# Moving the compressed softmax ahead of the attention loop, and two smaller moves, in a one-core hybrid S5 / sparse-attention layer

## The chip, the cores and the metric

The kernel runs on one core of one Trainium2 chip. The metric is device time in microseconds (us): 828.83 us is the median of three runs before the change (828.5 to 829.4). Matrix products, and the transposes that are done as products, run on TensorE (PE); VectorE is DVE, ScalarE ACT, GpSimd POOL, and SP issues most transfers.

## The reference

One layer on 512 tokens of width 1024, in float32:

```python
n1 = rmsnorm(h, g_mix);  z = n1 @ w_in
y_ssm = s5_mixer(z[:, :512], ...)                      # state space, gelu, glu gate
y_nsa = nsa_mixer(q, kv, gate_logits, ...)             # 8 heads of 64, 2 kv heads
#   o = gates[0]*o_cmp + gates[1]*o_sel + gates[2]*o_win
#   o_cmp: softmax over 31 compressed keys;  o_sel, o_win: causal softmax over 512 keys
merge = sigmoid(z[:, OFF_MERGE:])                      # 2 x 1024 columns
mixed = merge[:, :1024]*(y_ssm @ w_br_ssm) + merge[:, 1024:]*(y_nsa @ w_br_nsa)
h = h + mixed @ w_out
h = h + conv_ffn(rmsnorm(h, g_ffn))                    # 1024 -> 2 x 2816 -> 1024
h = h + sigmoid(rmsnorm(h, g_ple) @ w_ple_gate) * (p @ w_ple_proj)
return rmsnorm(h, g_final)
```

## The kernel before

Every large product is made of three in a reduced format: both operands are split into a high and a low part (`split`: ACT copies the high part, DVE or POOL subtracts it), and `mm3` (lines 83 to 85) issues high x high, high x low and low x high into one PSUM bank. So in the profile each weight tile shows an ACT copy (line 76), a subtraction (line 55) and three products on lines 83, 84, 85. PSUM has eight banks in four rings of two, named `acc`, `s`, `t` and `o`; a tile that is allocated takes the next bank of its ring and waits until that bank's earlier tile has been read. SBUF scratch goes the same way: the tag `mg` of pool `weights` is a ring of two.

The stages stand in program order: norm 1 and the input projections; the S5 quarters; the compressed keys and values (`compress`); the first four merge gates (`gate`, banks `acc`, tiles `pj`); the glu of the S5 output (tiles `glu`, then `sg`, `yg` in ring `mg`, then `y2`); attention; the rest of the merge; `w_out` (tiles `wo`); norm 2 (`norm`, and `to_t`, which transposes the normed rows into banks `nt` and evicts them as `n2h` and `n2l`); the FFN; the gated embedding; the final norm.

Attention is a loop over 16 units (8 heads, 2 branches), each of four steps. `scores` makes products `sps` on line 870, and the softmax runs over DVE, ACT, DVE and POOL (tile `pr`); `transposed` turns it on PE (tile `ptp`, line 885), and ACT and DVE split it into `ph` and `pl`; `values` makes the products on lines 896 to 900 into bank `ops`. The two branches of a head and its compressed part share one bank; at the end `otmp` and `oT` take the head's output out of it. Since these chains are long, a generator `fill` gives PE other work: the remaining 12 merge gates and the 8 products with `w_br_ssm`, 128 pieces (of three products each). `filled(n)` takes `n` pieces, and each step of the loop takes one. What is left is issued after the loop.

The compressed softmax (`compressed`, `compressed_t`) is done once per 128 queries for all heads: 12 products `cs` of 64 columns, eight small DVE and ACT steps on tile `cmps`, two transposes `pct`, and the split into `PTC`, which the first product of each head reads (lines 896, 897). It stands among the scores of the first unit.

The order on each engine is not the order of the text: a scheduler places the instructions by its own model of their times, and within one engine they then run strictly as placed. `tc.issue_after(x)` tells it to place what follows after instruction `x`. After the loop the head outputs `oT` are split into `oS` for the product with `w_br_nsa`; `oT` has one tile for two heads, so three of the four splits are ready before the last two heads are.

Of the kernel before, what the change touches and what calls it, by code (L numbers as in the profile page):

```python
# [9 lines left out]
F32 = mybir.dt.float32  # L10
# [8 lines left out]
P = 128  # L19
T = 512  # L20
# [25 lines left out]
def hybrid_kernel(ctx: ExitStack, tc: tile.TileContext, A, out):  # L46
# [7 lines left out]
    def tt(o, a, b, op, e=V):  # L54
        e.tensor_tensor(o, a, b, op=op)  # L55

    def ts(o, a, s1, s2=None, op0=MUL, op1=None, e=V):
        if op1 is None:
            e.tensor_scalar(o, a, s1, None, op0=op0)
        else:  # L60
            e.tensor_scalar(o, a, s1, s2, op0=op0, op1=op1)  # L61
# [16 lines left out]
    def split(hi, lo, src, e=V):  # L78
        copy(hi, src)
        tt(lo, src, hi, SUB, e)  # L80

    def mm3(ps, lh, ll, rh, rl, start, stop):
        PE.matmul(ps, lh, rh, start=start, stop=False)  # L83
        PE.matmul(ps, lh, rl, start=False, stop=False)  # L84
        PE.matmul(ps, ll, rh, start=False, stop=stop)  # L85
# [15 lines left out]
    def bank(tag, name):  # L101
        return psp.tile([P, 512], F32, tag=tag, name=name, bufs=BANKS[tag])

    def slot(p, tag, shape, dt, name):
        return p.tile(shape, dt, tag=tag, name=name, bufs=1)
# [5 lines left out]
    def small(tag, n=1, bufs=4):  # L111
        return cp.tile([P, n], F32, name=tag, tag=tag, bufs=bufs)
# [73 lines left out]
    def wload(name, ld, row0, c0, kt, c, e=V, keep=None, raw=None):  # L186
        if raw is None:
            raw = wraw(name, ld, row0, c0, kt, c)
        if keep is None:
            hi = pw.tile([P, kt * c], F32R, name="wh", tag="wh").rearrange("p (k c) -> p k c", k=kt)  # L190
            lo = pw.tile([P, kt * c], F32R, name="wl", tag="wl").rearrange("p (k c) -> p k c", k=kt)
        else:
            hi, lo = keep
        split(hi, lo, raw, e)
        return hi, lo
# [619 lines left out]
    def gate_weights(i, e=G):  # L815
        return wload("w_in", INW, 0, OFF_M + i * P, KD, P, e)

    for dt_ in range(4):
        for _ in gate(t1(dt_), gate_weights(dt_, (V, G)[dt_ % 2])):
            pass  # L820

    po = sY.enter_context(pool("att_out", 1, "right"))
    y2 = slot(po, "y16", [P, 2, 4, T], F32R, "y2")
# [4 lines left out]
        split(ys[:, 0, k], ys[:, 1, k], yT[:, k].rearrange("p j c -> p (j c)"))  # L828
    for hc in range(2):
        hi, lo = wload("ssm_w_glu", SSMW, 0, hc * 256, 4, 256, V)  # L830
        for cc in range(2):
            c = 2 * hc + cc
            ps = bank(either(), "glu")
            for k in range(4):
                mm3(ps, hi[:, k, cc * P:(cc + 1) * P], lo[:, k, cc * P:(cc + 1) * P], ys[:, 0, k], ys[:, 1, k],
                    k == 0, k == 3)
            sg, yg = (pw.tile([P, T], F32, name=n, tag="mg") for n in ("sg", "yg"))
            S.activation(sg, ps, AF.Tanh, scale=0.5)
            stt(yg.rearrange("p (c j) -> p j c", j=L), sg.rearrange("p (j c) -> p j c", j=L), 1.0, yT[:, c], ADD, MUL)
            split(y2[:, 0, c], y2[:, 1, c], yg)  # L840


    PTC = slot(pa, "ptc", [P, 2, 2, T], F32R, "PTC")
    oT = slot(py, "y8", [P, 4, T], F32, "oT")
    t1s.append(slot(po, "t16", [P, 4, T], F32, "t1b"))
    sB = ExitStack()
# [56 lines left out]
                copy(tmp, self.ops[64:128])  # L903
                tt(oT[self.r0:self.r0 + 64, self.i], self.ops[0:64], tmp, ADD)

    def compressed(qt):
        qs_ = slice(qt * P, (qt + 1) * P)
        ps = bank("s", "cs")
        for i in range(4):
            mm3(ps[:, 64 * i:64 * i + 64], QT[:, i, 0, qs_], QT[:, i, 1, qs_], KC[:, 0, i // 2], KC[:, 1, i // 2],  # L910
                True, True)
        sc = pt.tile([P, H, NCMP], F32, name="cmps", tag="cmps")
        shc = [P, H, NCMP]
        tt(sc, ps[:, 0:256].rearrange("p (h n) -> p h n", h=H), maskc[:, qt, None, :].to_broadcast(shc), ADD)
        mx, su = small("cmx", H, 2), small("csu", H, 2)
        V.tensor_reduce(mx, sc, AX.X, ALU.max)
        tt(sc, sc, mx[:, :, None].to_broadcast(shc), SUB)
        S.activation(sc, sc, AF.Exp, scale=HD ** -0.5)
        V.tensor_reduce(su, sc, AX.X, ADD)
        V.reciprocal(su, su)  # L920
        tt(su, su, gates[:, qt, 0:8], MUL)
        if qt == 0:
            ts(su, su, rowok)
        tt(sc, sc, su[:, :, None].to_broadcast(shc), MUL)
        return sc

    def compressed_t(qt, sc):
        pc = bank("t", "pct")
        for g in range(2):
            PE.transpose(pc[:, g * P:(g + 1) * P], sc[:, 4 * g:4 * g + 4].rearrange("p h n -> p (h n)"), ident)  # L930
        qs_ = slice(qt * P, (qt + 1) * P)
        split(PTC[:, 0, :, qs_], PTC[:, 1, :, qs_], pc[:, 0:256].rearrange("p (g t) -> p g t", g=2))

    def ssm_branch(dt_, w):
        ps = bank("acc", "br")
        c = (dt_ % 2) * P
# [36 lines left out]
    def filled(n):  # L973

        with tc.issue_after(last_pe()):
            for _ in range(n):
                next(fill, None)

    units = [Unit(h, br) for h in range(H) for br in range(2)]
    units[0].queries(None)  # L980
    scs = {}
    for qt in range(NQ):
        units[0].scores(NQ - 1 - qt)
        scs[qt] = compressed(qt)
        filled(4)
        if qt:
            compressed_t(qt - 1, scs[qt - 1])
    filled(4)
    compressed_t(NQ - 1, scs[NQ - 1])
    pend = None  # L990
    for n, u in enumerate(units):
        nxt = units[n + 1] if n + 1 < len(units) else None
        if nxt:
            nxt.queries(u)
        for i in range(NQ):
            kt = NQ - 1 - i
            u.transposed(kt)
            gate_at = last_pe()
            if pend:
                pend[0].values(pend[1], pend[2])  # L1000
            if nxt:
                nxt.scores(kt)
            pend = (u, kt, units[n - 1] if n else None)
            with tc.issue_after(gate_at):
                next(fill, None)
    pend[0].values(pend[1], pend[2])
    for _ in fill:
        pass

# [4 lines left out]
    w0h = pm_.tile([P, KD, 512], F32R, name="w0h")  # L1014
    hres = slot(cp, "h16", [P, NQ, D], F32, "hres")
    oS = slot(pa, "kv", [P, 2, 4, T], F32R, "oS")
    for i in range(4):
        split(oS[:, 0, i], oS[:, 1, i], oT[:, i])

    mTls = []  # L1020

# [42 lines left out]
    for qp in range(2):  # L1064
        for hf, qt in ((0, 0), (0, 1), (1, 0), (1, 1)) if qp == 0 else ((0, 2), (1, 2), (0, 3), (1, 3)):
            cs = slice(hf * 512, hf * 512 + 512)
            qs_ = slice(qt * P, (qt + 1) * P)
            ps = bank(either(), "wo")
            for k in range(KD):
                mm3(ps, mTh[:, k, qs_], mTl(k)[:, qs_], (w0h, w1h)[hf][:, k],  # L1070
                    w1l[:, k] if hf else w0l[k // 4][:, k % 4], k == 0, k == KD - 1)
            stt(hres[:, qt, cs], ps, 0.5, hres[:, qt, cs], MUL, ADD)
        for j in range(2):
            norm(xg[:, j], hres[:, 2 * qp + j])
        to_t([xg[:, j] for j in range(2)], 2 * qp, 0, lambda x, k, q, w: (n2h, n2l)[x][:, k, q * P:q * P + w])
    sY.close()
    sA.close()

# [451 lines left out]
```

## Time and profile before

| | us |
|---|---|
| three runs, median | 828.83 (828.5 to 829.4) |
| the profiled execution, device time | 829.46 |
| its span on the core | 827.5 |
| PE busy | 807.9 |
| DVE busy | 524.3 |
| ACT busy | 393.5 |
| POOL busy | 255.2 |

Busy time says how long an engine had something in it. On PE the records overlap: a product of 512 columns is shown as 0.39 us, while the next one starts 0.23 us after it. So a wait is read best from the starts of two neighbours, and the idle time that the profile prints in brackets is smaller than the gap between starts. [...]

### The profile page before, as it was taken

Reading aid. Unit: us, or ns where it says so; the run is one execution under the profiler, and the core shown is the slowest. Engines: PE = TensorE matmul, PEld = TensorE weight load, DVE = VectorE, ACT = ScalarE, POOL = GpSimd, SP = SyncE. Lnnn points to the kernel's source line nnn. Section 1 sums busy time; section 2 is a strip of 40 time slices with the busy share of each in tenths; the row PEclk is TensorE's granted clock in tenths of the full one; section 3 lists DMA queues with packets and bytes.
Section 4 is the critical chain, followed back from the end, with each engine's and each line's share of the span. In section 5 each row is a group of like instructions: output and inputs, shape, how many; then the busy total and the mean of one; then the engine's idle time right before and its main releaser. Section 6 shows DMA issues by size and latency. Waiting matters only on the chain. (4 is left out here: it accounts for less than half of the span.)

```text
span 827.5 us, 12241 instructions
## 1 busy us (share of the span) xinstructions
PE 807.9 (98%) x4529; PEld 677.7 (82%) x4529; DVE 524.3 (63%) x1088; ACT 393.5 (48%) x728; POOL 255.2 (31%) x314
## 2 busy tenths in 40 slices
PE   7999999999999999999999999999999999999996
PEld 5877888878888888888898888888888888888885
DVE  6899988377677640685454444444455947898744
ACT  4437553445777753434354444444434433565522
POOL 6595111124555533131032333333333100000411
PEclk9999999999999999999999999999999999999998
DMA  9663322522333423344052333233323342423011
GB/s 244 161 166 103 91 65 65 129 76 77 77 77 83 148 55 96 109 137 118 2 175 80 103 101 100 86 95 103 99 86 95 121 143 93 153 87 117 26 52 51
DMA packets 112001, 83.67 MB, mean 101 GB/s; under 512 B 9665, under 2 KB 97477, under 8 KB 111942
## 3 DMA queue, kind: packets, MB, share of 16 engines
q1 hardware_dynamic: 111262, 81.82, 34.2%
q10 hardware_dynamic: 680, 1.07, 0.3%
q8 instruction: 36, 0.59, 0.3%
q14 instruction: 23, 0.19, 0.1%
HBM read 75.54 MB, written 3.15 MB: 95 GB/s over the span
## 5 line engine op out<-in xcount | busy, mean ns | idle before, releaser
L55 POOL TENSOR_TENSOR wl<-wr,wh 128x1024 fp32r<-128x1024 f32 x39 | 93.6, 2401 | 246.5 <-ACT wh L76 228.5
L76 ACT ACTIVATE wh<-wr 128x1024 fp32r<-128x1024 f32 x90 | 95.2, 1059 | 95.5 <-issue 32.9
L55 DVE TENSOR_TENSOR wl<-wr,wh 128x1024 fp32r<-128x1024 f32 x51 | 66.0, 1294 | 42.7 <-ACT wh L76 42.7
L83 PE MATMUL pj<-n1h,wh 128*128 128x512 f32 x224 | 92.0, 411 | 0.3 <-ACT un L76 0.3
L85 PE MATMUL pj<-n1h,wl 128*128 128x512 f32 x224 | 88.9, 398 | 0.4 <-DVE wl L55 0.4
L84 PE MATMUL pj<-n1l,wh 128*128 128x512 f32 x224 | 88.6, 396 | 0.0
L64 DVE SCALAR_TENSOR_TENSOR cv<-ub,cvp,cv 128x511 f32<-128x511 f32 (+1 forms) x44 | 32.9, 748 | 66.3 <-ACT cv L1193 65.6
L84 PE MATMUL ua<-n2l,wh 128*128 128x512 f32 (+1 forms) x176 | 67.0, 381 | 0.4 <-DVE n2l L64 0.4
L83 PE MATMUL ua<-n2h,wh 128*128 128x512 f32 (+1 forms) x176 | 67.0, 380 | 0.2 <-ACT n2h L166 0.2
L83 PE MATMUL ub<-n2h,wh 128*128 128x512 f32 (+1 forms) x176 | 66.8, 379 | 0.0
L84 PE MATMUL ub<-n2l,wh 128*128 128x512 f32 (+1 forms) x176 | 66.8, 379 | 0.0
L85 PE MATMUL ub<-n2h,wl 128*128 128x512 f32 (+1 forms) x176 | 66.8, 379 | 0.0
L85 PE MATMUL ua<-n2h,wl 128*128 128x512 f32 (+1 forms) x176 | 66.8, 379 | 0.0
L85 PEld LDWEIGHTS pj<-n1h,wl 128*128 128x128 f32 x224 | 42.4, 189 | 10.3 <-DVE wl L55 1.1
L61 POOL TENSOR_SCALAR pr<-pr,su,gates 128x512 f32<-128x512 f32 (+1 forms) x64 | 38.3, 607 | 37.4 <-DVE su L877 36.3
L84 PEld LDWEIGHTS pj<-n1l,wh 128*128 128x128 f32 x224 | 42.7, 190 | 7.9 <-issue 0.6
L83 PEld LDWEIGHTS pj<-n1h,wh 128*128 128x128 f32 x224 | 42.6, 190 | 7.8 <-ACT un L76 0.6
L874 DVE CUSTOM_DVE_ANT_0 pr<-sps,maskb 128x512 f32<-128x512 f32 (+1 forms) x64 | 30.0, 487 | 18.8 <-PE sps L870 9.4
L55 POOL TENSOR_TENSOR wg1l<-wr,wg1h 128x1024 fp32r<-128x1024 f32 x2 | 7.0, 3514 | 111.5 <-ACT wg1h L76 111.5
L55 DVE TENSOR_TENSOR pl<-ptp,ph 128x128 fp32r<-128x128 f32 (+1 forms) x64 | 31.1, 486 | 14.5 <-ACT ph L76 13.8
L76 ACT ACTIVATE ph<-ptp 128x128 fp32r<-128x128 f32 (+1 forms) x64 | 27.6, 433 | 25.7 <-PE ptp L885 25.0
L84 PEld LDWEIGHTS ua<-n2l,wh 128*128 128x128 f32 x176 | 33.1, 188 | 6.8 <-DVE n2l L64 0.6
(495 smaller groups left out, 2078.0 us busy)
## 6 DMA issues: line engine op xcount, KB each, us to landing
wr<-in_w_up_dram SPq DMA_DIRECT2D x44, 512.0 KB, 3.9
wr<-in_w_in_dram SPq DMA_DIRECT2D x28, 512.0 KB, 4.0
b<-in_w_down_dram SPq DMA_DIRECT2D x12, 512.0 KB, 6.2
wr<-in_w_down_dram SPq DMA_DIRECT2D x10, 512.0 KB, 4.5
QQ<-QT SPq DMA_DIRECT2D x16, 256.0 KB, 3.4
wr<-in_w_out_dram SPq DMA_DIRECT2D x8, 512.0 KB, 4.4
wr<-in_w_ple_gate_dram SPq DMA_DIRECT2D x8, 512.0 KB, 5.3
xall<-in_x_dram SPq DMA_DIRECT2D x4, 512.0 KB
```

The lines of the kernel that those rows point to most:

```text
L55: e.tensor_tensor(o, a, b, op=op)
L61: e.tensor_scalar(o, a, s1, s2, op0=op0, op1=op1)
L64: e.scalar_tensor_tensor(o, a, s, b, op0=op0, op1=op1)
L76: S.activation(o, a, AF.Copy)
L83: PE.matmul(ps, lh, rh, start=start, stop=False)
L84: PE.matmul(ps, lh, rl, start=False, stop=False)
L85: PE.matmul(ps, ll, rh, start=False, stop=stop)
L874: V.tensor_tensor_reduce(out=pp, in0=ps[:, :w], in1=maskb[:, T - w:], scale=-(HD ** -0.5), scalar=3e38, op0=ADD, op1=ALU.min, accum_out=nb)
```

## The change

Three parts. `compressed` and `compressed_t` move up, textually unchanged, to the loop over the first four gates: after each gate stand the 12 products and the softmax of one query tile, and the transposes of the tile before; the last transposes come after the first glu weights. The scratch `cmps` changes from a ring of its own in the attention pool to the ring `mg`, and `PTC` is allocated earlier. In attention, the first unit's scores now take three pieces of filling each and no more (12 instead of 20), the last unit takes two pieces a step instead of one, and the splits of `oT` are ordered after the last head's output. In norm 2 the second pair of query tiles is transposed into four different banks (`t`, `t`, `acc`, `o`) instead of the two of ring `t` in turn. Line numbers of the changed program are some 4 to 36 higher: `sps` is on line 906, `pct` on 845, `ptp` on 921, the products of `values` on 932 to 936.

```diff
     for dt_ in range(4):
         for _ in gate(t1(dt_), gate_weights(dt_, (V, G)[dt_ % 2])):
             pass
+        scs[dt_] = compressed(dt_)
+        if dt_:
+            compressed_t(dt_ - 1, scs[dt_ - 1])
...
+    def compressed(qt):
...
+        sc = pw.tile([P, H, NCMP], F32, name="cmps", tag="mg")
...
     for hc in range(2):
         hi, lo = wload("ssm_w_glu", SSMW, 0, hc * 256, 4, 256, V)
+        if hc == 0:
+            compressed_t(NQ - 1, scs[NQ - 1])
...
-        sc = pt.tile([P, H, NCMP], F32, name="cmps", tag="cmps")
...
     for qt in range(NQ):
         units[0].scores(NQ - 1 - qt)
-        scs[qt] = compressed(qt)
-        filled(4)
-        if qt:
-            compressed_t(qt - 1, scs[qt - 1])
-    filled(4)
-    compressed_t(NQ - 1, scs[NQ - 1])
+        filled(3)
...
             with tc.issue_after(gate_at):
-                next(fill, None)
+                for _ in range(1 if nxt else 2):
+                    next(fill, None)
     pend[0].values(pend[1], pend[2])
+    attended = [last(e) for e in (mybir.EngineType.DVE, mybir.EngineType.Activation)]
...
-    for i in range(4):
-        split(oS[:, 0, i], oS[:, 1, i], oT[:, i])
+    with tc.issue_after(attended[0]), tc.issue_after(attended[1]):
+        for i in range(4):
+            split(oS[:, 0, i], oS[:, 1, i], oT[:, i])
...
-        to_t([xg[:, j] for j in range(2)], 2 * qp, 0, lambda x, k, q, w: (n2h, n2l)[x][:, k, q * P:q * P + w])
+        to_t([xg[:, j] for j in range(2)], 2 * qp, 0, lambda x, k, q, w: (n2h, n2l)[x][:, k, q * P:q * P + w],
+             tags=("t", "t", "acc", "o") if qp else "tttt")
```

The program holds the same products and transposes as before. Three places in its order, before and after:

First, PE around the second full group of `cs` in the program before; then the place in the changed one where a group stands between two gates (a line of dots stands for more rows of the same kind).

```order
L85 MATMUL pj<-n1h,wl 128x512
L870 MATMUL sps<-KK,QQ 128x256 x2
L83 MATMUL cs<-KC,QT 128x64
...
L83 MATMUL pj<-n1h,wh 128x512
L930 MATMUL pct<-ident,cmps 128x128 x2
```

```order
L84 MATMUL pj<-n1l,wh 128x512
L845 MATMUL pct<-ident,cmps 128x128 x2
L85 MATMUL pj<-n1h,wl 128x512
L83 MATMUL cs<-KC,QT 128x64
...
L845 MATMUL pct<-ident,cmps 128x128 x2
L83 MATMUL pj<-n1h,wh 128x512
```

Before, the groups stand 12 gate products apart (2.8 us at 0.23 us each), with scores between; now they stand 18 and 24 gate products apart, and the scores come after the glu.

Second, ACT around the last two heads, from the first `ph` of the last head's first unit, before and then changed. `oS` are the copies of finished heads, `otmp` takes out the head before, `ph` is what the products of `values` wait for.

```order
L76 ACTIVATE ph<-ptp 128x128
L76 ACTIVATE oS<-oT 128x512 x3
L876 ACTIVATE pr_3831,su<-pr_3831,nb 128x128
L76 ACTIVATE otmp<-ops 64x512
L76 ACTIVATE ph<-ptp 128x256
```

```order
L76 ACTIVATE ph<-ptp 128x128
L912 ACTIVATE pr_3799,su<-pr_3799,nb 128x128
L76 ACTIVATE otmp<-ops 64x512
L76 ACTIVATE ph<-ptp 128x256
...
L76 ACTIVATE otmp<-ops 64x512
L76 ACTIVATE oS<-oT 128x512 x3
```

The three copies have moved from before the `ph` of 256 columns to behind the very last `otmp`. On DVE the three subtractions have moved with them.

Third, PE at norm 2's last transposes, before and then changed; the number at `nt` is the bank's tile.

```order
L163 MATMUL nt_4620<-ident_69,xg_4299 128x128 x3
L163 MATMUL nt_4629<-ident_69,xg_4299 128x128 x3
L83 MATMUL ua_4675<-n2h_4297,wh_4665 128x256
L83 MATMUL ub_4676<-n2h_4297,wh_4671 128x256
L84 MATMUL ua_4675<-n2l_4298,wh_4665 128x256
...
L163 MATMUL nt_4638<-ident_69,xg_4299 128x128 x4
...
L163 MATMUL nt_4647<-ident_69,xg_4299 128x128 x4
```

```order
L163 MATMUL nt_4620<-ident_69,xg_4299 128x128 x3
L163 MATMUL nt_4629<-ident_69,xg_4299 128x128 x3
L163 MATMUL nt_4638<-ident_69,xg_4299 128x128 x3
L163 MATMUL nt_4647<-ident_69,xg_4299 128x128 x3
L83 MATMUL ua_4675<-n2h_4297,wh_4665 128x256
L83 MATMUL ub_4676<-n2h_4297,wh_4671 128x256
L84 MATMUL ua_4675<-n2l_4298,wh_4665 128x256
```

Six transposes in a row have become twelve (and 6 us earlier, where each bank's first transpose stands, two have become four); the two groups of four that stood between the FFN products are gone.

## Rows read from the trace of the kernel before

**Rows 1.** The page: busy time, share of the span and instructions of each engine.

```profile
PE 807.9 (98%) x4529; PEld 677.7 (82%) x4529; DVE 524.3 (63%) x1088; ACT 393.5 (48%) x728; POOL 255.2 (31%) x314
```

**Rows 2.** Stretches: length, each engine's busy time; last, clock, DMA share, GB/s.

```profile
180.00:200.00 20.00, 19.10 (x103) 16.26 (x102) 16.53 (x45) 8.58 (x21) 8.87 (x7) 0.91 0.17 54
...
280.00:300.00 20.00, 19.23 (x112) 16.29 (x112) 14.09 (x47) 15.18 (x40) 8.82 (x12) 1.00 0.12 30
...
400.00:420.00 20.00, 19.38 (x143) 18.08 (x142) 7.58 (x21) 8.48 (x17) 1.58 (x1) 1.00 0.01 2
420.00:760.00 340.00, 340.00 (x1550) 283.57 (x1550) 200.05 (x291) 151.34 (x214) 79.49 (x55) 1.00 0.36 111
```

**Rows 3.** What PE waited for: us in total, times, longest.

```profile
PE cs L83 <- DVE cmps L55: 0.9, 1, 0.9
```

**Rows 4.** PE in time order at 183 to 191: start, us, what, [idle before].

```profile
183.63 0.39 PE L85 MATMUL pj<-n1h,wl 128*128 128x512 f32 x1
183.85 0.40 PE L870 MATMUL sps<-KK,QQ 128*128 128x256 f32 x2
185.15 0.30 PE L83 MATMUL cs<-KC,QT 128*128 128x64 f32 x1 [0.90 <-DVE cmps L55]
...
187.28 0.61 PE L85 MATMUL pj<-n1h,wl 128*128 128x512 f32 x1
...
190.93 0.40 PE L85 MATMUL pj<-n1h,wl 128*128 128x512 f32 x1
```

**Rows 5.** PE alone by the microsecond: busy, then granted clock, DMA.

```profile
188.00:189.00 1.00, 1.00 (x4) 0.50 0.00 0
...
396.00:397.00 1.00, 1.00 (x11) 1.00 0.00 0
```

**Rows 6.** All engines in time order at 293.9 to 297.7, the last head's first unit.

```profile
293.90 1.68 ACT L76 ACTIVATE oS<-oT 128x512 fp32r<-128x512 f32 x3
...
294.57 2.00 DVE L55 TENSOR_TENSOR oS<-oT,oS 128x512 fp32r<-128x512 f32 x3
...
296.13 0.40 PE L85 MATMUL pj<-n1h,wl 128*128 128x512 f32 x1
...
296.61 0.77 ACT L76 ACTIVATE ph<-ptp 128x256 fp32r<-128x256 f32 x2
...
297.04 0.38 PE L899 MATMUL ops<-ph,VV 128*128 128x256 f32 x1 [0.51 <-ACT ph L76]
...
297.68 0.39 PE L900 MATMUL ops<-pl,VV 128*128 128x256 f32 x1 [0.26 <-DVE pl L55]
```

**Rows 7.** PE, ACT and DVE in time order at norm 2's transposes.

```profile
395.87 1.03 PE L163 MATMUL nt<-ident,xg 128*128 128x128 f32 x8
...
410.33 0.82 PE L163 MATMUL nt<-ident,xg 128*128 128x128 f32 x6
410.86 1.57 ACT L166 ACTIVATE n2h<-nt,gains 128x256 fp32r<-128x256 f32 x4 [2.24 <-PE nt L163]
411.73 1.66 DVE L64 SCALAR_TENSOR_TENSOR n2l<-nt,gains,n2h 128x256 fp32r<-128x256 f32 x4 [3.35 <-ACT n2h L166]
```

**Rows 8.** PE alone, the same place.

```profile
411.61 0.28 PE L83 MATMUL ub<-n2h,wh 128*128 128x256 f32 x1
412.27 0.39 PE L84 MATMUL ua<-n2l,wh 128*128 128x256 f32 x1 [0.38 <-DVE n2l L64]
...
413.09 0.60 PE L163 MATMUL nt<-ident,xg 128*128 128x128 f32 x4
413.45 0.36 PE L84 MATMUL ua<-n2l,wh 128*128 128x256 f32 x1
```

**Rows 9.** DVE and ACT in time order, one glu output leaving its bank.

```profile
168.56 1.08 DVE L64 SCALAR_TENSOR_TENSOR yg<-sg,yT 128x512 f32<-128x512 f32 x1 [1.29 <-ACT sg L838]
...
169.67 0.63 ACT L76 ACTIVATE y<-yg 128x512 fp32r<-128x512 f32 x1 [1.14 <-DVE yg L64]
...
170.34 0.69 DVE L55 TENSOR_TENSOR y<-yg,y 128x512 fp32r<-128x512 f32 x1 [0.70 <-ACT y L76]
```

More of the change, by code (lines that the diff above doesn't have):

```diff
@@ L816, in gate_weights, with compressed_t @@
         return wload("w_in", INW, 0, OFF_M + i * P, KD, P, e)
+    PTC = slot(pa, "ptc", [P, 2, 2, T], F32R, "PTC")
+    def compressed(qt):
+        qs_ = slice(qt * P, (qt + 1) * P)
+        ps = bank("s", "cs")
+        for i in range(4):
+            mm3(ps[:, 64 * i:64 * i + 64], QT[:, i, 0, qs_], QT[:, i, 1, qs_], KC[:, 0, i // 2], KC[:, 1, i // 2],
+                True, True)
+        sc = pw.tile([P, H, NCMP], F32, name="cmps", tag="mg")
+        shc = [P, H, NCMP]
+        tt(sc, ps[:, 0:256].rearrange("p (h n) -> p h n", h=H), maskc[:, qt, None, :].to_broadcast(shc), ADD)
+        mx, su = small("cmx", H, 2), small("csu", H, 2)
+        V.tensor_reduce(mx, sc, AX.X, ALU.max)
+        tt(sc, sc, mx[:, :, None].to_broadcast(shc), SUB)
+        S.activation(sc, sc, AF.Exp, scale=HD ** -0.5)
+        V.tensor_reduce(su, sc, AX.X, ADD)
+        V.reciprocal(su, su)
+        tt(su, su, gates[:, qt, 0:8], MUL)
+        if qt == 0:
+            ts(su, su, rowok)
+        tt(sc, sc, su[:, :, None].to_broadcast(shc), MUL)
+        return sc
+    def compressed_t(qt, sc):
+        pc = bank("t", "pct")
+        for g in range(2):
+            PE.transpose(pc[:, g * P:(g + 1) * P], sc[:, 4 * g:4 * g + 4].rearrange("p h n -> p (h n)"), ident)
+        qs_ = slice(qt * P, (qt + 1) * P)
+        split(PTC[:, 0, :, qs_], PTC[:, 1, :, qs_], pc[:, 0:256].rearrange("p (g t) -> p g t", g=2))
+    scs = {}
     for dt_ in range(4):
@@ L840, in hybrid_kernel @@
             split(y2[:, 0, c], y2[:, 1, c], yg)
-    PTC = slot(pa, "ptc", [P, 2, 2, T], F32R, "PTC")
     oT = slot(py, "y8", [P, 4, T], F32, "oT")
@@ L904, in values @@
                 tt(oT[self.r0:self.r0 + 64, self.i], self.ops[0:64], tmp, ADD)
-    def compressed(qt):
-        qs_ = slice(qt * P, (qt + 1) * P)
-        ps = bank("s", "cs")
-        for i in range(4):
-            mm3(ps[:, 64 * i:64 * i + 64], QT[:, i, 0, qs_], QT[:, i, 1, qs_], KC[:, 0, i // 2], KC[:, 1, i // 2],
-                True, True)
-        sc = pt.tile([P, H, NCMP], F32, name="cmps", tag="cmps")
[L913 to L932, printed above, removed]
     def ssm_branch(dt_, w):
@@ L980, in hybrid_kernel @@
     units[0].queries(None)
-    scs = {}
     for qt in range(NQ):
         units[0].scores(NQ - 1 - qt)
-        scs[qt] = compressed(qt)
-        filled(4)
-        if qt:
-            compressed_t(qt - 1, scs[qt - 1])
-    filled(4)
-    compressed_t(NQ - 1, scs[NQ - 1])
+        filled(3)
     pend = None
@@ L1016, in hybrid_kernel @@
     oS = slot(pa, "kv", [P, 2, 4, T], F32R, "oS")
-    for i in range(4):
-        split(oS[:, 0, i], oS[:, 1, i], oT[:, i])
+    with tc.issue_after(attended[0]), tc.issue_after(attended[1]):
+        for i in range(4):
+            split(oS[:, 0, i], oS[:, 1, i], oT[:, i])
     mTls = []
```

## The prediction

> **What bounds the kernel now.** I read the page's busy shares first: PE is busy 807.9 of 827.5 us [rows 1], so the kernel is as long as its chain of products, and a change can gain only where PE waits, runs at half clock, or does avoidable work. Then the stretches [rows 2]: from 420 to 760 PE has no idle time at the full clock, so what is gained before 420 arrives at the end, unless something behind it depends on absolute times; DVE's 200 and ACT's 151 of those 340 us leave room. In the stretches that the change touches, PE misses 0.90 us in 180 to 200, 0.77 in 280 to 300 and 0.62 in 400 to 420, and only the first has a granted clock under 1.00 (0.91). Everything lies in these three stretches.
>
> The list of waits [rows 3] and the timeline [rows 4] explain the first: the second full group of `cs` stands 12 gate products behind the first, finds its bank still unread because DVE is late with `cmps` (DVE is busy 16.5 of these 20 us), and PE starts nothing from about 183.97 to 185.15. Two us later the products slow down: the clock is 0.50, its lower level [rows 5], and before the fall PE had done that wait and then 12 products of only 64 columns.
>
> **The first place.** The wait: second `sps` of 256 columns at about 183.97, 0.12 us long at 0.23 per 512 columns (183.63 to 183.85), next start 185.15 [rows 4]: 1.06 us. The half clock: nine starts from 187.28 to 190.93 take 3.65 us; nine at 0.23 take 2.07: 1.58 us. In the new order the groups stand 18, 24 and 24 gate products (4.1 to 5.5 us) apart, and no score uses ring `s` between them, so DVE has to read a bank some 9.6 to 11 us before it is needed again, not 2.8. No product disappears; the compressed work on DVE and ACT moves to a place where those engines wait for PE. I take both gains whole, 2.64 us. Bounds: nothing (the wait turns up elsewhere) and 2.64.
>
> What stands behind the moved work on its engines: on ACT, the high parts of gate 4's and the glu's weights now queue behind the exponentials. PE wants gate 4's tile 42 products after the first group (18 of gate 2, 24 of gate 3: 9.7 us at 0.23). Ahead of its copy stand three steps of `cmps`, none longer than the 0.69 of a DVE step on 512 columns [rows 9], a table load that stood there before as well, and behind it POOL's subtraction. That covers it, and if it didn't, PE would wait in the fourth gate. On SP only two small pairs of transfers change places; the first `QQ` go out before all of this as they did.
>
> Twenty filling pieces become twelve at the start, eight in place of four in the last unit, and four more stay for behind the loop: same work, at no cost as long as there is something to fill with.
>
> **The last head.** ACT spends 1.68 us and DVE 2.00 us on three `oS` splits while the last head's chain needs them [rows 6]. From the product at 296.13 to that at 297.04 are 0.91 us, not 0.23: 0.68 lost, to `ph`. From 297.04 to 297.68 are 0.64, not 0.12 (256 columns): 0.52 lost, to `pl`. The splits move behind the last `otmp`, and the product that needs them stands over 120 gate products later (28 us at 0.23), while four splits take some 5 us. Without them `ph` would start up to 1.68 us earlier than at 296.61, 0.5 us earlier than PE asks. Gain 1.20 us; bounds 0.5 (if `otmp` alone still holds `ph` up) and 1.3.
>
> **Norm 2.** Four transposes hold PE 0.36 us (413.09 to 413.45), and the product behind them is 0.08 longer (0.36 for 0.28) [rows 8]. Two such groups leave the FFN's first products: 0.88. Two transposes more at the early place cost 0.18, and everything up to 412.27 shifts by as much. The other six go into gaps that PE has anyway: three transposes still fill the first bank, so its eviction starts 0.53 us after the first of them (410.33 to 410.86), `n2l` 0.87 later, and the product at 412.27 can't come sooner [rows 7, 8]. Gain 0.88 - 0.18 = 0.70; bounds 0 and 0.9. The `acc` and `o` banks were last used by products for tile 2, long read. ACT and DVE evict a k-tile in about 0.4 us each (1.57 and 1.66 for four); PE uses one per 0.72 us (six products of 0.12), so the third and fourth bank are no worry.
>
> [...] The trace had eight in a row at 395.87 [rows 7], and the clock stayed 1.00 [rows 5]. [...]
>
> **Fewer breaks.** A 512-column product directly behind transposes or `cs` starts its successor 0.08 late (0.36 for 0.28 above is the same effect). In the two orders I count 72 such places before and 69 after: 0.24 us; the transposes of the convolution weights, split in two before, now stand together, one break less. I take 0.3, with 0 and 0.5 as bounds.
>
> **Sum:** 2.64 + 1.20 + 0.70 + 0.30 = 4.84 us of the profiled execution's 829.46. That execution is 0.63 above the median of the runs shown, so for the median: 828.83 - 4.84 = 824.0 us. A change below 0.2% (1.7 us) can't be told from none here.
>
> **Rivals.**
>
> A, the half clock stays. Neither the 0.77 nor the 0.62 us of idle time dropped the clock [rows 2], so waits of that size have stood without a fall; what PE did beside the wait here were the 64-column products, and these stay, the first group now right behind the many small products of the S5 stage. Or it falls at the twelve transposes. Against it: no wait now lies beside either. Price 1.58: 825.6 us.
>
> B, a smaller gain stays out: the last head's `ph` is late because of `otmp` and the exponential before it, which remain on ACT. For it: they end right before `ph`. Against: the loop's other heads show no such wait. Price 1.2: 825.2 us.
>
> C, A and B together, or A with a new wait of about 1.5 us in the first unit, whose scores now come after the glu and so nearer to their transposes: 4.84 - 1.58 - 1.5 leaves 1.8, and less if norm 2 gives nothing: 827 to 828.8, no change that could be told.
>
> D, slower: the ring `mg`. `sg` and `yg` of the glu share its two buffers with `cmps`, and the first `yg` can't be written before the last `pct` has read `cmps`, nine products before the glu's end. From then on the four outputs leave one after the other: 1.08 + 0.63 + 0.69 and some 0.1 of handing over, 2.5 us each [rows 9]. The last bank is free three such turns, one `yg` and one `sg` (put at 0.63, as the other ACT step) later, 9.2 us; PE asks for it behind 33 products of 512 columns (7.6) and the scores and first head products between (about 2.1): 9.7 us. It decides from 0.5 us on. In its worst form (two score steps on DVE and a weight copy on ACT stand between, at 0.69, 0.69 and 1.08 by their nearest rows [rows 9], and the ring serves one output at a time, a turn of 2.5 more) PE waits 4.5 us, four times the wait that goes, and loses two stretches of half clock (3.2): 7.7 against 4.84 gained, 2.9 slower: 831.7 us. Against it: the orders on DVE and ACT put `yg` first, and the outputs' later half overlaps; a wait under 1 us costs only that.
>
> **How the numbers follow.** Forecast 0.62 (its own range 822.8 to 825.0, from the bounds of norm 2, the breaks and the last head). A 0.15, B 0.08, C 0.09, D 0.06, counted whole on the slow side. Faster by over 0.2%: forecast, A and B, 0.85. Same: C, 0.09. Slower: D, 0.06. The range that leaves out C, D and little more reaches from 822.8 to A with a loss of half a wait beside it, 826.3.
>
> **What would show it.** Right: PE's wait list without `cs` and `ops`; clock 1.00 from 20 to 800 us; PE idle under 0.4 us in the norm 2 place, with the wait for `n2l` as its only entry; span near 822.5. Wrong: a stretch of clock 0.50 between 148 and 420; a PE wait on `sg` or `PTC` at the first `ops` or the second filling gate (D); a wait for `ph` in the last head (B). Should PE be idle for the same total and the time the same, the gain would have been taken back behind 420, which I exclude by its full rows.

## The result, and the profile after

| | before | changed |
|---|---|---|
| median of 4 runs each, us | 829.04 (828.5 to 829.4) | 824.67 (824.54 to 824.73) |
| ratio, 95% interval | | 0.9948 [0.993, 0.9965] |
| the profiled execution, us | 829.46 | 824.63 |
| its span, us | 827.5 | 822.9 |
| PE busy, us | 807.9 | 805.5 |

The changed kernel is faster by 4.4 us of medians, 4.83 us of profiled executions. The forecast was 824.0, and the measured time lies in its range. The forecast's sum of 4.84 is met within 0.01 by the two profiled executions, which is in part luck, and its error of 0.67 is in the base that the sum was taken from, as the experiments show. One run of the kernel before, of 60 beside the experiments, took 4600.1 us and is left out of all that follows.

The page's busy line of the changed kernel answers to [rows 1]:

```profile
PE 805.5 (98%) x4529; PEld 676.6 (82%) x4529; DVE 522.0 (63%) x1088; ACT 392.6 (48%) x728; POOL 255.7 (31%) x314
```

The stretches, with the columns of [rows 2]: length, then busy time of PE, PEld, DVE, ACT and POOL, then the granted clock, DMA share and GB/s. The granted clock is what the profile prints as a share of TensorE's full speed. By the microsecond, the profile of before has it at 1.00 in 818 of the first 826, at 0.50 in five and between the two in three (at 187, 190 and 822), where it changes; half clock means the 0.50.

```profile
180.00:200.00 20.00, 20.00 (x104) 16.86 (x103) 14.89 (x40) 13.95 (x34) 10.90 (x11) 1.00 0.38 105
...
280.00:300.00 20.00, 20.00 (x113) 17.07 (x112) 8.71 (x27) 11.36 (x27) 8.57 (x10) 1.00 0.21 54
...
400.00:420.00 20.00, 19.77 (x165) 19.47 (x164) 10.90 (x24) 11.48 (x19) 4.91 (x2) 1.00 0.27 78
420.00:760.00 340.00, 339.65 (x1533) 282.12 (x1533) 200.20 (x296) 152.05 (x220) 76.16 (x53) 1.00 0.35 107
```

The first two places are full now, and the clock is 1.00 where it was 0.91 on the mean. Norm 2 keeps 0.23 us of its 0.62. The 0.35 that PE misses behind 420 is one wait (for `hres`, below) that fell behind 760 in the earlier program; it came nearer with everything else and is no loss. In the list of waits `cs` and `ops` are gone, and these are what remains behind the merge gates (us in total, times, longest):

```profile
PE pj L83 <- DVE hres L55: 0.3, 1, 0.3
PE ua L84 <- DVE n2l L64: 0.2, 1, 0.2
```

Where the 4.8 us went is read from the starts of the same products in both traces. The last `kps`, ahead of everything changed, starts at 148.47 before and 148.40 now. The first `wo`, behind attention, starts at 358.29 and 354.13: 4.09 gained between them. The last product of all starts at 819.16 and 814.35: 4.81, so norm 2 brought the rest, and nothing was given back or won between it and the last product.

The last head in time order on ACT and PE: start, duration, what, idle time before it in brackets.

```profile
294.83 0.49 ACT L76 ACTIVATE ph<-ptp 128x384 fp32r<-128x384 f32 x1 [1.99 <-PE ptp L921]
...
298.96 0.34 PE L935 MATMUL ops<-ph,VV 128*128 128x384 f32 x1
...
303.48 1.66 ACT L76 ACTIVATE oS<-oT 128x512 fp32r<-128x512 f32 x3
```

The `ph` of 384 columns is ready at 295.32, 3.6 us before PE uses it, and the `oS` splits that stood in front of such a step [rows 6] come behind the head. Norm 2 on PE answers to [rows 7, 8]:

```profile
406.40 1.47 PE L163 MATMUL nt<-ident,xg 128*128 128x128 f32 x12
407.63 0.36 PE L83 MATMUL ua<-n2h,wh 128*128 128x256 f32 x1
407.83 0.28 PE L83 MATMUL ub<-n2h,wh 128*128 128x256 f32 x1
408.34 0.38 PE L84 MATMUL ua<-n2l,wh 128*128 128x256 f32 x1 [0.23 <-DVE n2l L64]
```

Twelve transposes stand together, and the two groups of four that cut into the first FFN products are gone. The clock through them, by the microsecond (length, PE busy, granted clock, DMA share, GB/s):

```profile
406.00:407.00 1.00, 1.00 (x11) 1.00 0.00 0
407.00:408.00 1.00, 1.00 (x11) 1.00 0.00 0
```

### The profile page after: what moved, and what is told of

It is laid out like the page before. It is cut to its first block, busy times and chain, and to the rows that moved or that the text cites. A ratio compares the mean times of both kernels' runs of the same rounds, so it can differ in the third digit from the quotient of the medians.

```text
span 822.9 us, 12250 instructions
## 1 busy us (share of the span) xinstructions
PE 805.5 (98%) x4529; PEld 676.6 (82%) x4529; DVE 522.0 (63%) x1088; ACT 392.6 (48%) x728; POOL 255.7 (31%) x314
## 5 line engine op out<-in xcount | busy, mean ns | idle before, releaser
L912 ACT ACTIVATE pr<-pr,nb 128x512 f32<-128x512 f32 (+1 forms) x64 | 35.6, 556 | 7.3 <-DVE nb L910 7.2
```

The source lines that it names most:

```text
L912: S.activation(pp, pp, AF.Exp, bias=nb, scale=-1.0, accum_out=su)
```

## The experiments

Twelve kernels ran in three groups of four, each group on one chip beside the kernel before. One fact is needed to read the times: the runs of the kernel before fall into two groups. Of the 59 beside these experiments, 33 lie from 828.09 to 828.68 (median 828.46), 24 from 829.15 to 829.67 (median 829.36) and two between. The first set shows why.

### One part at a time

The compressed softmax moved, the other two parts undone:

```diff
-                for _ in range(1 if nxt else 2):
-                    next(fill, None)
+                next(fill, None)
...
-    with tc.issue_after(attended[0]), tc.issue_after(attended[1]):
-        for i in range(4):
-            split(oS[:, 0, i], oS[:, 1, i], oT[:, i])
+    for i in range(4):
+        split(oS[:, 0, i], oS[:, 1, i], oT[:, i])
...
-             tags=("t", "t", "acc", "o") if qp else "tttt")
```

> The changed kernel with its last two parts undone: the compressed softmax stands beside the gates and three filling products stand between the first scores, but the last head is filled once per step, the `oS` splits stand where they stood, and norm 2 evicts from one ring. Theory (the forecast's terms): 2.64 us for the wait and the half clock and about 0.2 of the 0.3 for breaks, so 2.8 to 2.9 us less than before (about 826.2 where before takes 829.0); no `cs` in PE's list of waits, clock 1.00 from 20 to 800 us, the last head's `ops` waits and norm 2's idle 0.62 as before. Rival (the place is worth more or less than the sum of rows says, and the other two parts make up for it): under 2.3 or over 3.4 us less.

Only the `oS` splits later, in the kernel before:

```diff
-    for i in range(4):
-        split(oS[:, 0, i], oS[:, 1, i], oT[:, i])
+    with tc.issue_after(attended[0]), tc.issue_after(attended[1]):
+        for i in range(4):
+            split(oS[:, 0, i], oS[:, 1, i], oT[:, i])
```

> The kernel before, with only the four `oS` splits put behind the last head's own work on DVE and ACT; the filling of the last unit stays at one piece per step and PE's order is the same. Theory (the `oS` splits are what makes the last head late): 1.20 us less than before, PE idle in 280 to 300 falls from 0.77 to under 0.1. Rival B1 (`otmp` alone holds `ph` up): 0.5 us less or nothing, with `ops` still in PE's list of waits. Rival B2 (the doubled filling is what covers the chain): nothing less, the same 0.77 us idle.

Only the filling of the last unit doubled, in the kernel before:

```diff
-                next(fill, None)
+                for _ in range(1 if nxt else 2):
+                    next(fill, None)
```

> The kernel before, with only the filling of the last unit doubled (two pieces per step, so eight products more between its steps); the `oS` splits stand where they stood. Theory (the splits make the last head late, and more filling gives the chain more time while it lasts): between 0 and 0.7 us less than before, with part of the idle time in 280 to 300 left. Rival B2 (the filling alone covers it): 1.2 us less, no idle time left, and the splits' place is then worth nothing.

Only norm 2's four banks, in the kernel before:

```diff
+             tags=("t", "t", "acc", "o") if qp else "tttt")
```

> The kernel before, with only the second half of norm 2's transposes put into four banks. Theory: two groups of four transposes with their breaks leave the first FFN products, two transposes more stand early: 0.65 to 0.70 us less than before, PE idle in 400 to 420 falls from 0.62 to 0.2 or 0.3, clock 1.00 through twelve transposes in a row. Rival (the transposes only change place): no change within 0.2 us. Rival (the clock falls behind twelve transposes): about 0.9 us more than before, with a stretch of 0.50 behind 410.

Measured, beside 828.49 for the kernel before:

| kernel | median, us | ratio, 95% interval | groups of runs |
|---|---|---|---|
| compressed moved | 826.45 | 0.9973 [0.9963, 0.9983] | 8 runs within 826.35 to 826.58 |
| splits later | 827.43 | 0.9987 [0.9978, 0.9996] | 8 about 827.41, 3 above 827.9 |
| more filling | 828.98 | 1.0007 [0.9998, 1.0016] | 6 about 828.74, 5 about 829.66 |
| four banks | 827.83 | 0.9992 [0.9983, 1.0] | 9 about 827.78, 2 about 828.78 |

The kernels that keep the compressed softmax at its old place keep the split into groups; the one that moves it has a spread of 0.23 us. The profiled execution with four banks (827.96) is one of its lower group, that with more filling (829.70) one of its upper. At the compressed groups both programs have the same order, and PE reads, with four banks:

```profile
186.50 0.48 PE L83 MATMUL pj<-n1h,wh 128*128 128x512 f32 x1
...
189.55 0.33 PE L870 MATMUL sps<-KK,QQ 128*128 128x128 f32 x2
190.22 0.44 PE L930 MATMUL pct<-ident,cmps 128*128 128x128 f32 x2 [0.33 <-DVE cmps L55]
190.61 0.30 PE L83 MATMUL cs<-KC,QT 128*128 128x64 f32 x1
```

and with more filling:

```profile
186.50 0.74 PE L83 MATMUL pj<-n1h,wh 128*128 128x512 f32 x1
187.05 0.63 PE L930 MATMUL pct<-ident,cmps 128*128 128x128 f32 x2
```

Up to 186.50 the two agree within 0.02 us, the 1.06 us wait for `cs` included. Then one is at half clock and the other isn't. By the microsecond, with four banks:

```profile
187.00:188.00 1.00, 1.00 (x7) 1.00 0.00 0
188.00:189.00 1.00, 1.00 (x6) 1.00 0.00 0
```

and with more filling:

```profile
187.00:188.00 1.00, 1.00 (x5) 0.50 0.00 0
188.00:189.00 1.00, 1.00 (x4) 0.50 0.00 0
```

So the fall of the clock in the profile of before is not a property of the program but something that its wait brings in about two runs of five, and the two groups of times are runs with it and without. The mean granted clock of each run bears that out: in the group of 33 it is 0.996 to 0.998 in every run, in the group of 24 it is 0.994 or 0.995 in all but one (829.24, at 0.998). Nor is the fall worth the 1.58 us of slower products: where it doesn't come, PE reaches the next `pct` before `cmps` is ready. From the `sps` at 189.55 to `cs` at 190.61 are 1.06 us, against 0.33 (191.16 to 191.49) in the profile of before: 0.73 lost to a wait that the half clock had hidden. The third `cs` group starts at 191.49 with the fall and 190.61 without, so the fall costs 0.88, and the groups of runs stand 0.90 apart.

What makes DVE late in both places can be read as well, from DVE and POOL in the kernel before:

```profile
179.29 2.38 POOL L55 TENSOR_TENSOR wl<-wr,wh 128x1024 fp32r<-128x1024 f32 x1 [5.20 <-ACT wh L76]
180.16 2.45 DVE L64 SCALAR_TENSOR_TENSOR yg<-sg,yT 128x512 f32<-128x512 f32 x1
184.72 0.37 DVE L55 TENSOR_TENSOR cmps<-cs,maskc 128x256 f32<-128x256 f32 x1
```

and from DVE with four banks:

```profile
187.61 2.55 DVE L55 TENSOR_TENSOR cmps<-cmps,csu 128x256 f32<-128x256 f32 x1
```

The `yg` step ahead of the `cmps` that frees the bank takes 2.45 us, where it takes 1.08 without a POOL step beside it [rows 9]: 1.37 more, and the wait is 1.06. The `cmps` step ahead of the late `pct` takes 2.55, and 0.42 at 185.93 in the same profile; a POOL step of 2.39 us starts at 187.49. So DVE is not only busy there, it is held up by subtractions of weights on POOL (more at the end of this document). By these rows both waits would have gone without the hold; that is an estimate, as no run moved a POOL step.

With that the parts can be priced, like against like. **Compressed moved:** 826.45 is 2.91 under the runs with the fall (2.8 to 2.9 was expected of them) and 2.01 under those without. **Splits later:** 827.41 against 828.46, 1.05, where 1.20 was expected; in 280 to 300 nothing is missing:

```profile
280.00:300.00 20.00, 20.00 (x118) 17.19 (x116) 12.32 (x43) 14.41 (x37) 10.00 (x13) 1.00 0.10 28
```

That settles the cause of the last head's waits: the splits, not `otmp` (rival B) and not too little filling. **More filling** alone leaves that stretch as it was:

```profile
280.00:300.00 20.00, 19.24 (x112) 16.29 (x111) 14.07 (x47) 15.18 (x40) 8.81 (x12) 1.00 0.12 31
```

The waits stand in the last head's first unit, and the doubled filling comes with its second. This kernel is even 0.3 us slower in both groups, though its last product starts at 819.20, within 0.05 of before's; 0.2 lies behind all computing. The chain of waits ends, in the kernel before, with

```profile
823.37 0.72 ACT xf L1489
```

and with more filling with

```profile
823.40 0.72 ACT xf L1490
```

and the spans end 3.4 us (827.5) and some 3.6 us (827.8) after that step. **Four banks:** 827.78 against 828.46, 0.68, with the clock at 1.00; 0.65 to 0.70 was expected:

```profile
400.00:420.00 20.00, 19.77 (x152) 18.88 (x151) 8.79 (x21) 9.31 (x19) 2.50 (x1) 1.00 0.14 40
```

The three gains sum to 2.01 + 1.05 + 0.68 = 3.74 us from the runs without the fall; the changed kernel lies 828.46 - 824.67 = 3.79 below them. The parts add up to within a few tenths, and no closer than that can be said: the doubled filling, which alone cost 0.3, is not in the sum, and the lower group's median differs by up to 0.17 between the chips (828.44, 828.61, 828.46).

### Place or distance

The old place with seven filling pieces between the groups:

```diff
     for qt in range(NQ):
         units[0].scores(NQ - 1 - qt)
         scs[qt] = compressed(qt)
-        filled(4)
+        filled(7)
```

> The kernel before, with seven filling pieces in place of four between the compressed groups of the first unit, so that 19 to 21 gate products stand between two full groups of `cs` where 12 stood; everything else, the place included, as before, and the later units have the fewer pieces left. Theory (what pays is the distance between the groups, not the place; and the clock falls only behind a wait beside the 64-column products): no `cs` in PE's list of waits, none of the runs with the stretch of clock 0.50, so a time close to the lower of the two times that before shows (828.4) less 1.1 for `cs` and 0.5 for the `pct` wait: 826.8, and as much more as units that now lack filling lose. Rival (the short products by themselves bring the fall): the spread of about 1 us between runs stays, and profiles show 0.50 behind a group without any wait. Rival (the old place has another wait behind the first, as POOL, DVE or ACT is late there anyway): `cs` goes and a wait for `ph`, `pct` or `sps` of the same size appears.

The new place without the distance, and the changed kernel with a single piece of filling, and the changed kernel once more:

```diff
         for _ in gate(t1(dt_), gate_weights(dt_, (V, G)[dt_ % 2])):
             pass
+    for dt_ in range(4):
         scs[dt_] = compressed(dt_)
```

> The changed kernel, with the compressed groups of the first merge taken out from between the gates and all four issued behind the last gate, so that the full groups stand 24, 10 and 2 products apart beside the glu in place of 18, 24 and 24. Theory (distance pays): `cs` is back in PE's list of waits with 1 to 3 us for the last two groups, and the time is 1 to 4 us more than the changed kernel's (825.7 to 828.7); with such waits beside the 64-column products the clock may fall again in some runs. Rival (the place alone pays, DVE has time there whatever the distance): the changed kernel's time within 0.3, no `cs` wait.

```diff
-                for _ in range(1 if nxt else 2):
-                    next(fill, None)
+                next(fill, None)
```

> The changed kernel, with the filling of the last unit back at one piece per step; the `oS` splits stay behind the last head's own work. Theory (the splits were the cause, the doubled filling covers nothing that is left): no `ops` in PE's list of waits, 280 to 300 without idle time, and the time of the changed kernel within 0.3 us; if the program's last instructions take 8.35 us behind the last product in place of 8.55, as in every kernel measured so far whose last unit is filled singly, 0.2 less: 824.4. Rival (in the new order the chain of the last head needs the doubled filling): 0.3 to 1.2 us more and `ops` waits again.

> The changed kernel once more, beside the three others on the same chip: 824.7 with a spread of about 0.2 between runs, no stretch of clock 0.50 between 20 and 800 us; if the fall of the clock can come in this kernel too, some runs about 1 us above the others.

Measured, beside 829.29 for the kernel before (most of its runs here had the fall):

| kernel | median of runs, us | ratio, 95% interval |
|---|---|---|
| old place, seven pieces | 826.04 (825.81 to 826.08) | 0.9963 [0.9949, 0.9976] |
| new place, close | 828.80 (827.79 to 830.27) | 0.9997 [0.9988, 1.0006] |
| single filling | 824.82 (824.72 to 825.17) | 0.9948 [0.9936, 0.9961] |
| changed | 824.67 (824.58 to 825.5) | 0.9948 [0.9935, 0.996] |

**Seven pieces at the old place** do what the move did, and a little more (826.8 was expected, so they came out 0.76 better): neither `cs` nor `pct` is waited for, the five runs lie within 0.27 us, and 180 to 200 is full at clock 1.00:

```profile
180.00:200.00 20.00, 20.00 (x112) 17.13 (x111) 16.67 (x38) 9.04 (x19) 8.67 (x7) 1.00 0.24 80
```

The 64-column products are all there, so they alone don't bring the fall; the rival that said so is out. The last head's wait for `ph` is gone too, which the expectation had not counted: between the transposes at 300.94 and the products that need that `ph`, at 307.01, PE now has filling, and `ph` is ready at 303.73. A wait for a gate's output has come:

```profile
PE pj L83 <- ACT t L813: 0.5, 1, 0.5
```

**Close at the new place.** The size came out just over the range expected, and the mechanism was another: `cs` isn't waited for. But `cmps` has two buffers in ring `mg`, so the last two softmaxes start only when a `pct` has freed one, DVE idling for it, and the last `pct` comes behind the glu instead of in its middle. That is rival D's chain. DVE and PE in time order:

```profile
173.83 0.42 DVE L55 TENSOR_TENSOR cmps<-cs,maskc 128x256 f32<-128x256 f32 x1 [2.93 <-PE pct L845]
...
181.42 0.60 PE L845 MATMUL pct<-ident,cmps 128*128 128x128 f32 x4
...
183.04 2.30 DVE L64 SCALAR_TENSOR_TENSOR yg<-sg,yT 128x512 f32<-128x512 f32 x1
```

The last `pct` was at 178.72 in the changed kernel; the first `yg` ends at 185.34 instead of 180.28. Of these 5.06 us the late `pct` is 2.70; another 1.22 is that `yg` takes 2.30 and not 1.08, beside a POOL step of 2.37 us that starts at 182.03. The scores' softmax steps queue behind it on DVE, and PE waits 1.5 us for a bank of `sps`, as its list of waits says:

```profile
PE sps L907 <- DVE nb L911: 1.5, 1, 1.5
```

There the clock falls. PE alone by two microseconds (length, PE busy, granted clock, DMA share, GB/s):

```profile
184.00:186.00 2.00, 0.49 (x2) 0.77 0.18 46
186.00:188.00 2.00, 2.00 (x9) 0.50 0.63 220
```

This execution took 830.27 and is the slowest of eleven (mean granted clock 0.993; 0.998 in the two fastest, so the fall is not in all of them); the median is 4.1 us above the changed kernel's. So the new place is no advantage in itself. It helps only while the last `pct` is early.

**Single filling** is 0.15 slower than the changed kernel, within the 0.3 of the theory: no `ops` wait, no idle time in 280 to 300. The 824.4 that the theory would have had by a shorter end was missed. Its path to the first `wo` is 0.29 longer in its profile (206.02 from the last `kps`, against 205.73). Some 0.23 of that is one place: the four transposes of the convolution weights near 309.5 stand in two pairs, each with a 512-column product behind it that has its successor 0.33 us later and not 0.23, as in the kernel before; in the changed kernel the four stand together. The end behind the last product is 8.4 us, 8.55 in the changed kernel, which takes half of that back. The doubled filling is worth about 0.1 us here, and not because it covers a wait. Of the changed kernel's 14 runs over three groups one, at 825.5, lies more than 0.2 above 824.67; I have no profile of it.

### The slack of rival D, and the better order

Rival D's chain, lengthened: the first glu output's `yg` is computed twice, with the same result.

```diff
-            stt(yg.rearrange("p (c j) -> p j c", j=L), sg.rearrange("p (j c) -> p j c", j=L), 1.0, yT[:, c], ADD, MUL)
+            for _ in range(2 if c == 0 else 1):
+                stt(yg.rearrange("p (c j) -> p j c", j=L), sg.rearrange("p (j c) -> p j c", j=L), 1.0, yT[:, c], ADD, MUL)
```

> The changed kernel, with the first glu output's step `yg` done twice on DVE (1.08 us more in the chain behind the last `pct`, the result the same). Theory (rival D's chain of glu outputs is real and has about 0.5 us of slack before PE asks for the last bank): PE waits some 0.6 us in the first unit, time 0.4 to 0.8 us more than the changed kernel's, or up to 1.8 if the clock falls behind it in some runs. Rival (the outputs overlap, the slack is larger than 1.08): no PE wait, the same time within 0.2.

And the old place with more distance, together with the later splits and the four banks, the filling of the last unit single:

```diff
-        filled(4)
+        filled(6)
```

> The kernel before with the compressed softmax at its old place, but six filling pieces between its groups (16 to 18 gate products between two full groups), the `oS` splits behind the last head's own work, the filling of the last unit single, and the four banks at norm 2. Theory (distance pays, wherever the groups stand, and 16 to 18 products are enough): the seven-piece kernel's 826.0 less 0.65 for norm 2 and 0 to 0.5 for the wait for `t` behind the last head, so 824.9 to 825.4; no `cs` wait. Rival (the new place is worth something of its own): 825.5 or more. If 16 products fall short, `cs` or `pct` is back with a few tenths.

The same with `filled(7)`, and the changed kernel beside them:

> As the kernel with six pieces, with seven (19 to 21 gate products between two full groups). Theory: 824.9 to 825.4, no `cs` wait, the wait for `t` gone if the `oS` splits on ACT were its cause, 0.5 left if the filling that the later units lack is its cause. If it beats the changed kernel's 824.7 by over 0.2, distance at the old place is the better edit.

> The changed kernel beside the three others: 824.7 within 0.2.

Measured, beside 828.69 for the kernel before (14 runs):

| kernel | median of runs, us | ratio, 95% interval |
|---|---|---|
| longer first output | 825.39 (825.32 to 825.47) | 0.9959 [0.9946, 0.9972] |
| old place, six | 826.32 (825.84 to 827.89) | 0.9974 [0.9965, 0.9982] |
| old place, seven | 824.25 (824.20 to 824.39) | 0.9945 [0.9931, 0.996] |
| changed | 824.67 (824.36 to 824.77) | 0.9949 [0.9936, 0.9962] |

**The longer output** costs 0.72 us, within the 0.4 to 0.8 expected, but the bank that PE waits for is the second output's and not the last's. In the changed kernel, ACT, PE and DVE in time order show how near that is:

```profile
179.20 1.08 DVE L64 SCALAR_TENSOR_TENSOR yg<-sg,yT 128x512 f32<-128x512 f32 x1 [5.55 <-PE pct L845]
...
180.85 0.58 ACT L875 ACTIVATE sg<-glu 128x512 f32<-128x512 f32 x1
...
182.31 0.40 PE L83 MATMUL pj<-n1h,wh 128*128 128x512 f32 x1
```

DVE waits 5.55 us for the last `pct`, as D said. The second bank is read at 181.43 and wanted at 182.31: 0.88 us of slack. With the longer output:

```profile
182.10 0.40 PE L934 MATMUL ops<-PTC,VC 128*128 128x512 f32 x1
...
182.11 0.58 ACT L875 ACTIVATE sg<-glu 128x512 f32<-128x512 f32 x1
...
182.74 0.50 PE L83 MATMUL pj<-n1h,wh 128*128 128x512 f32 x1 [0.25 <-ACT sg L875]
```

The read moves by 1.26 us; less 0.88 that leaves 0.38, and PE loses 0.41 (0.64 between starts, not 0.23). By the first `wo` its profile is 0.54 behind the changed kernel's; for the rest of the 0.72 between the medians I have no row.

**Six pieces** are not enough. The `cs` bank is free in time, but the next step of the same chain is late:

```profile
PE pct L930 <- DVE cmps L55: 1.2, 1, 1.2
```

Again a step of the chain runs beside a POOL step. POOL and DVE, ahead of that `pct` at 187.98:

```profile
185.06 2.38 POOL L55 TENSOR_TENSOR wl<-wr,wh 128x1024 fp32r<-128x1024 f32 x1 [1.29 <-ACT wh L76]
185.11 2.35 DVE L59 TENSOR_SCALAR csu<-csu,rowok 128x8 f32<-128x8 f32 x1
```

A step of eight elements a partition, 0.22 us in the kernel before, takes 2.35 and ends with POOL's. Less these 2.13 the wait of 1.2 would have gone, by estimate. Three of its eleven runs lie 1.6 us above the other eight, and their mean granted clock is 0.995 where the others have 0.997 or 0.998; the profile is one of the eight and has 1.00 at this place. The kernel missed the expectation of 824.9 to 825.4.

**Seven pieces** give the chain time for that as well, the same step of 2.35 us included, and with the splits later the wait for `t` is gone (PE is busy all of 300 to 360):

```profile
180.00:200.00 20.00, 20.00 (x112) 17.15 (x111) 16.84 (x40) 9.06 (x19) 8.66 (x7) 1.00 0.25 80
...
300.00:360.00 60.00, 60.00 (x277) 49.02 (x276) 34.88 (x43) 25.64 (x42) 21.12 (x11) 1.00 0.33 107
```

At 824.25, 0.65 under the range expected, this is the lowest median of all, 0.42 below the changed kernel on the same chip; its highest run, 824.39, is just above the other's lowest, 824.36, and the two intervals overlap. From the last `kps` to the first `wo` it takes 205.51 us, the changed kernel 205.73, and the end behind the last product is 8.34 against 8.55. So one number and two of the three parts do as well as the move, or slightly better, without the coupling of `cmps` to the glu through ring `mg`.

## Why the prediction was right, and where it was off

**The base.** The step that failed is the last line of the sum: "That execution is 0.63 above the median of the runs shown, so for the median: 828.83 - 4.84". The 4.84 hold 1.58 us of half clock that only some runs have, and the median mixes runs of both kinds. The profiled execution is one with the fall, and the changed kernel has none, so the sum had to stay with that execution: 829.46 - 4.84 = 824.62. Measured were 824.63 in the profile and 824.67 as the median. That 4.84 and 4.83 agree within 0.01 is luck in part: the terms measured below differ from the forecast's by up to 0.15, three profiled executions of the changed kernel lie from 824.36 to 824.67, and the span shrank by 4.6 only, the other 0.2 lying outside of it. The span, forecast near 822.5, is 822.9; 0.2 of that is the longer end behind the last computing step. Three runs 0.3 to 0.6 apart were taken for noise about one value. The forecast's own range, 822.8 to 825.0, does not follow from its bounds either: taken whole from 828.83 they give 823.5 to 825.7. The measured time lies in both.

**The first place, 2.64.** Right for executions with the fall: 2.91 measured with the breaks, 2.64 and about 0.2 to 0.3 forecast. Without the fall it is 2.01, since a wait of 0.73 us for `pct` stands where the half clock stood. I had no term for that wait, because the profile that I read could not show it. The forecast's reason, distance between the groups, is shown both ways: with distance at the old place the waits go, and without it at the new place the gain is lost. Its reading of why DVE is late, that it is busy 16.5 of these 20 us, was incomplete: part of that time is the steps held up beside POOL.

**The last head, 1.20.** Measured 1.05 by the runs. The cause was the one named. The two pieces of filling a step, which I put at no cost, cost 0.3 alone and are worth about 0.1 net in the changed kernel.

**Norm 2, 0.70.** 0.68 alone, 0.64 by the starts in the changed kernel (4.80 gained at the 512-column `ua` products behind it, where the first `wo` had 4.16). A fall of the clock at the twelve transposes, the other form of rival A, did not come. In the trace the clock is 1.00 from 406 to 408, and over all of 400 to 420.

**Fewer breaks, 0.30.** 2.91 less 2.64 leaves 0.27, a remainder and not a measurement of its own. One of its places can be read: the transposes of the convolution weights, standing together, save some 0.23 and not the 0.08 of one break. They stand together in the changed kernel and in pairs in the one with only the compressed softmax moved, so the 0.27 doesn't hold them.

**The rivals.** A, the half clock stays: three profiles of the changed kernel have 1.00 from 20 to 760, and the short products without the wait bring no fall. My evidence against A was right (no wait lies beside them), but it missed that the fall was a matter of chance already. B fell with the experiment on the splits. Nothing of C came. D, the ring `mg`, is a real mechanism: DVE does wait 5.55 us for the last `pct`. I put 0.5 us of slack at the last bank; it is 0.88 at the second. That "a wait under 1 us costs only that" was an estimate: waits of 0.73 us (four banks) and 0.41 (longer output) stood at clock 1.00, and the shortest behind which a fall is seen is the 1.06. The price, with the last `pct` 2.7 us later, was 4.1 us, less than the 7.7 of its worst form.

## What to carry to other kernels

Where runs of a kernel fall into groups, find out which group the profile is from before you subtract anything from a median: a stall that is priced from the trace has to be taken from that execution's time. When a bank is late because its reader's chain is long, try more independent work between its users first; it is one number, and it was worth as much as a move that tied the chain to another ring. Look at the next wait in the same chain too: six pieces freed the bank and left `pct` late by 1.2 us. And before making room for a late chain, look whether its steps take their usual time: here a DVE step of 0.22 us took 2.35 beside a POOL step, and giving POOL's step another place or engine, which was not tried, might have done as much as the distance.

## What the runs showed of the hardware

The clock can fall or stay behind the same instructions. Two executions with equal starts up to 186.50 went on at 0.50 (more filling) and at 1.00 (four banks). It fell behind a wait of 1.06 us followed by 64-column products, and also, in the close kernel, behind one of 1.5 us beside score products of 256 to 512 columns.

Some DVE steps with their operands in SBUF took longer beside a POOL step. In the changed kernel:

```profile
182.46 2.57 POOL L55 TENSOR_TENSOR wl<-wr,wh 128x1024 fp32r<-128x1024 f32 x1 [3.71 <-ACT wh L76]
...
182.71 0.70 DVE L910 CUSTOM_DVE_ANT_0 pr<-sps,maskb 128x512 f32<-128x512 f32 x1
...
183.79 1.79 DVE L55 TENSOR_TENSOR y<-yg,y 128x512 fp32r<-128x512 f32 x1
```

The `y` step, 0.69 us elsewhere [rows 9], takes 1.79 and ends 0.55 us after POOL's, while the step on `sps`, which has one operand in PSUM, runs beside POOL unhindered (0.70 us; 0.69 in the close kernel before POOL starts). The 2.30 and 2.45 us of `yg` above, against 1.08, the 2.55 of `cmps`, against 0.42, and the 2.35 of `csu`, against 0.22, are the same. At `y` POOL starts first, at 182.46, and DVE's step, which starts at 183.79, ends only behind it. By what mechanism is not shown.

What ends a program behind its last computing step took 3.4 to 3.5 us in the kernel before, with the compressed softmax moved, with the splits later, with the single filling and with seven pieces and the other two parts, and 3.6 in the changed kernel and some 3.6 with more filling. What makes the difference was not tried.
